# First half of the second FFN: 13 of 22 f-tiles by seven products of block sums in place of eight

## The chip, the core and the metric

One core of one Trainium2 chip runs the kernel. The metric is device time in microseconds, from one launch. The core has five engines that run side by side, each through its own instructions in a fixed order: TensorE (PE, matmuls and transposes; its weight loads are listed as PEld), VectorE (DVE), ScalarE (ACT), GpSimd (POOL) and SyncE (SP), which here only issues DMA transfers. Engines wait for each other by semaphores.

## The reference

The kernel computes one layer of a diffusion backbone on 512 latent tokens and 256 context tokens of width 1024. The change lies in its last part, the second feed-forward layer on the latent tokens, all in fp32:

```python
def ffn_sublayer(h, m, i, w_up, w_down):
    shift, scale, gate = sub_mod(m, i)
    y = swiglu(modulate(h, shift, scale), w_up, w_down)
    return post_ln(DEEPNORM_ALPHA * h + 0.5 * gate * y, ln_g[i], ln_b[i])

def swiglu(u, w_up, w_down):
    a, b = jnp.split(u @ w_up, 2, axis=-1)
    return (jax.nn.silu(a) * b) @ w_down
...
x = post_ln(DEEPNORM_ALPHA * x + gate_x * branch_merge(...), ln_g[1], ln_b[1])
...
x = ffn_sublayer(x, mod_x, 2, ffn2_w_in, ffn2_w_out)
```

`modulate` is a layer norm with scale and shift. The hidden width is D_FF = 2816, which is 22 f-tiles of 128.

## The kernel before

Every fp32 matrix product is made of three products of rounded parts: `split` makes of a tile a high part (a cast to fp32r on ACT) and a low part (the difference, on DVE), and a product is high x high + high x low + low x high. So a product over 1024 channels is 8 x 3 = 24 matmuls with a 128x128 weight tile held still and the tokens moving.

The part around the change runs like this. The output projection w_o of the mixers is a call of `down` (line 186) over four token tiles t of 128; behind the last matmul of each token tile `finish2` (L1319) scales the result by the gate, adds ALPHA times the residual x1, which it loads from the DRAM tensor x1d into a tile xr (L1321, two buffers), applies a layer norm with weights (`post_ln`, L248 and L249) and keeps the result as x2 in SBUF, four tiles. Then `ln_norm` makes from x2 the normalised y(t): statistics on DVE, the power on POOL (L104, L108, L123), the scaling on ACT (L124). `u3` transposes y(t) on PE (`to_u`, L139), adds scale and shift on ACT (L142) and splits it into the token columns of uxh and uxl, the moving operand of the second FFN.

The first half of the second FFN then runs f-tile by f-tile: two weight tiles of 128x1024 (one for a, one for b) are loaded by `Stream`, split, and used by `ffn_unit` (24 matmuls each, then silu and product in `glu`, then the split of the result into hh and hl). The first NH = 4 f-tiles run in two halves of 256 tokens, so that PE can begin when the first two token tiles are there: first the lower half of all four, in between `u3` for token tiles 2 and 3, then the upper halves. The other 18 run with 512 tokens. The second half of the FFN, `down` again, takes hh and hl as still operands and the rows of w_down as moving ones; after it come gate, residual x2 and the last layer norm, token tile by token tile.

The order of instructions on each engine is set when the kernel is built: a scheduler of the tile framework orders the program by its own estimates of cost, and each engine then runs its list strictly in that order. Buffers of one name are handed out again when the last reader of the old contents is done.

Of the kernel before, what the change touches and what calls it, by code (L numbers as in the profile page):

```python
# [17 lines left out]
P = 128  # L18
D = 1024
# [38 lines left out]
def body(ctx, tc, I, out, dbg=None):  # L58
# [73 lines left out]
    def to_u(tp, pp, xn, uh, ul, c0, scale, shift):  # L132

        u32 = tl(tp, [P, KT, P], "u32")
        for hb in range(2):
            ps = tl(pp, [P, 4, P], "ps", 8)
            for q in range(4):
                k = hb * 4 + q
                T.transpose(ps[:, q, :], xn[:, k * P:(k + 1) * P], ident)  # L139
# [4 lines left out]
            split(u32[:, ks], uh[:, ks, c0:c0 + P], ul[:, ks, c0:c0 + P])  # L144

# [40 lines left out]
    def down(pp, ws, hs, ntt, kl, pre=(), between=None, after=None, pieces=0, post=()):  # L186
# [6 lines left out]
        def one(i, t, wh, wl, cols=((0, 0, 512), (1, 0, 512)), first=None, last=None):  # L193
            hh, hl = hs[i]
            if first is None:
                first, last = done[t] == 0, done[t] == len(hs) - 1
                done[t] += 1
            sl = slice(t * P, (t + 1) * P)
            for j, (a, b) in enumerate(((hh, wh), (hh, wl), (hl, wh))):
                for d, c0, c1 in cols:  # L200
                    T.matmul(banks[t][d][:, c0:c1], a[:, sl], b[:, d * 512 + c0:d * 512 + c1], start=first and j == 0, stop=last and j == 2)  # L201

        n = len(hs) - len(pre) - len(post)
# [47 lines left out]
    def ffn_unit(tp, pp, A, B, uh, ul, n, hh, hl):  # L251
# [4 lines left out]
        glu(tp, pa, pb, n, hh, hl)  # L256

    def glu(tp, pa, pb, n, hh, hl):
        s = tl(tp, [P, NX], "fs", 2)
        S.activation(s[:, 0:n], pa[:], AF.Silu)  # L260
        V.tensor_tensor(s[:, 0:n], s[:, 0:n], pb[:], ALU.mult)  # L261
        split(s[:, 0:n], hh[:, 0:n], hl[:, 0:n])
# [37 lines left out]
    def secs(col, s):  # L300
        return col[:, s * 8:s * 8 + 8]
# [988 lines left out]
    PMB[:] = "pm", 4  # L1290
    wb, close_wb = pool("w3", "right")
# [18 lines left out]
    x2p, close_x2p = pool("x2")  # L1310
    x2 = [tl(x2p, [P, D], f"x2{t}") for t in range(4)]
    up, close_up = pool("u3")
    uxh = tl(up, [P, KT, NX], "uxh", 1, F32R)
    uxl = tl(up, [P, KT, NX], "uxl", 1, F32R)
    lp, close_lp = pool("l3")
# [3 lines left out]
    def finish2(t, banks):  # L1319
        xr = tl(lp, [P, D], "xr", 2)  # L1320
        nc.sync.dma_start(xr[:], x1d[t])  # L1321
        h = x2[t]
        for d in range(2):
            sl = slice(d * 512, (d + 1) * 512)
            V.tensor_tensor(h[:, sl], banks[d][:], gx[:, sl], ALU.mult)
            V.scalar_tensor_tensor(h[:, sl], xr[:, sl], ALPHA, h[:, sl], op0=ALU.mult, op1=ALU.add)
        post_ln(lp, h, lng, lnb)
        if "x2" in dbg:
            nc.sync.dma_start(dbg["x2"][t * P:(t + 1) * P, :], h[:])
        y = tl(lp, [P, D], "y1", 2)  # L1330
        ln_norm(lp, y[:], h, act=True)
        return y

    def u3(t, y):
        to_u(lp, pp, y, uxh, uxl, t * P, secs(colx, 7), secs(colx, 6))
# [9 lines left out]
    JU, FU = 2, (1, 3)  # L1345
# [5 lines left out]
    NH = 4  # L1351
    h2a, close_h2a = pool("h2a", "right")
    wc, close_wc = pool("w4", "right")
    hs = []
    key = lambda j: ("", "", "b", "b", "b", "b", "c", "c")[j] if j < 2 * NH else "" if j % 6 in (1, 2) else "b"
    src = [I["up2"][i] for i in range(2 * NF)] + rows(I["dn2"], range(NF))
    ws = Stream(wp, [(w, key(j)) if key(j) else w for j, w in enumerate(src)], WB, 2)
    ws.extra = {"b": (wb, 4, wp, WB), "c": (wc, 2, wp, WB)}
# [7 lines left out]
    hh0 = [h2(h2a, NH) for _ in range(NH)]  # L1366
# [8 lines left out]
    close_wc()  # L1375
    close_lp()
    hp2, close_hp2 = pool("h2", "right")
# [3 lines left out]
    close_tp()  # L1381
    close_up()
# [3 lines left out]
    lng, lnb = load_ln(lp, 2)  # L1386
    PIECES = 2
    banks, _ = down(pp, ws, hs, 4, KL2, pieces=PIECES)
    for t in range(4):
        h = tl(lp, [P, D], "h4", 2)  # L1390
        n, m = (512, D) if t < 3 else (D // PIECES, 512)
        st = tl(lp, [P, PIECES, 6], "bst", 4)
        for i, c in enumerate(range(0, D, n)):
            sl = slice(c, c + n)
            V.tensor_tensor(h[:, sl], banks[t][c // 512][:, c % 512:c % 512 + n], gx[:, sl], ALU.mult)
            V.scalar_tensor_tensor(h[:, sl], x2[t][:, sl], ALPHA, h[:, sl], op0=ALU.mult, op1=ALU.add)
            V.bn_stats(st[:, i, :], h[:, sl])
# [6 lines left out]
        for c in range(0, D, m):  # L1404
            sl = slice(c, c + m)
            V.scalar_tensor_tensor(h[:, sl], h[:, sl], rs[:, 0:1], lnb[:, sl], op0=ALU.mult, op1=ALU.add)
            nc.sync.dma_start(out[t * P:(t + 1) * P, sl], h[:, sl])
    close_lp()
    close_hp2()
    close_h2a()  # L1410
    close_wb()
    close_x2p()
# [102 lines left out]
```

## Time and profile before

| | us |
|---|---|
| median of 3 runs (1559.4 to 1562.53) | 1561.29 |
| the profiled execution | 1563.3 |
| its span, first to last instruction | 1561.2 |
| mean granted clock of TensorE, of full speed | 0.984 |
| w_o by `down`, first L201 matmul at | 1141.5 |
| second FFN, lower and upper halves of four f-tiles, from | 1187.6 |
| the other 18 f-tiles, from | 1236.4 |
| the down projection, from | 1432.3 |

A row of a view in order of time has the start, the duration, the engine, the line, the operation, what it writes and reads with shapes, how many instructions were merged (x2), and in brackets how long the engine was idle before it and which instruction ended that. A row of busy time by stretches has the stretch, its length, then busy time and instruction count of PE, PEld, DVE, ACT and POOL, the granted clock, the share of DMA time and GB/s. Names are those of the program without buffer numbers and trailing digits (u32 is shown as u, x2 as x). A matmul's duration counts its way through the array; in a stream, the distance between starts is what one costs.

### The profile page before, as it was taken

The page shows a single profiled execution, that of the slowest core. Times are in us where ns is not written, and L with a number is a line of the kernel's source. Part 1 is how long each engine was busy: PE and PEld are TensorE (multiplying, and loading weights), DVE is VectorE, ACT ScalarE, POOL GpSimd, SP SyncE. Part 2 cuts the span into 40 slices and gives each one's busy share as a digit, 9 for nine tenths or more (in the row PEclk, how much of TensorE's full clock was granted, in tenths as well). Part 3 has the DMA queues.
Part 4 walks back from the last instruction along what each step waited for, and adds up shares of the span by engine and source line. Part 5 has one row for each costly group of instructions (what it writes and reads, how often), then busy time and mean ns, then how long its engine had stood idle before and what let it go on. Part 6 is the DMA issues. An engine that isn't in the chain of part 4 may idle for free.

```text
span 1561.2 us, 22187 instructions
## 1 busy us (share of the span) xinstructions
PE 1488.2 (95%) x8681; PEld 1252.0 (80%) x8681; DVE 932.0 (60%) x1567; ACT 569.0 (36%) x941; POOL 199.8 (13%) x236
## 2 busy tenths in 40 slices
PE   6999999999999999999996899999799999999997
PEld 4778988888888888889875788867579988888886
DVE  7666762587545487758777795576578333333226
ACT  5434321222112255555543444265426322222110
POOL 1000000000000022223301001376432000000001
PEclk9999999999999999999998999999999999999999
DMA  8665562556555434222476634272252322323221
GB/s 314 201 212 193 181 197 94 196 182 204 195 183 187 164 108 146 85 85 83 137 221 169 172 92 119 88 281 95 90 180 95 96 95 96 103 99 135 95 81 54
DMA packets 106427, 226.43 MB, mean 145 GB/s; under 512 B 34049, under 2 KB 47697, under 8 KB 106321
## 3 DMA queue, kind: packets, MB, share of 16 engines
q1 hardware_dynamic: 105888, 223.89, 43.9%
q8 instruction: 68, 1.11, 0.3%
q10 hardware_dynamic: 434, 1.12, 0.2%
q14 instruction: 37, 0.30, 0.1%
HBM read 204.23 MB, written 20.75 MB: 144 GB/s over the span
## 4 chain that ended last, share of the span: by engine, by line
PE 65%; DMA 12%; DVE 11%; issue 6%; ACT 3%; POOL 2%; SPq 1%; DVEq 0%; POOLq 0%; ACTq 0%
PE ps L201 20%; PE ps L184 8%; PE ps L182 8%; PE ps L183 8%; DMA wr<-in_w_adaT_dram 7%; PE pm L182 4%; PE pm L183 4%; PE pm L184 4%; DVE wl L130 3%; PE pc L842 2%; DVE adap L268 2%; PE po L1250 1%; DMA Dt<-gcd 1%; PE pt L1239 1%; DVE bt L939 1%
## 5 line engine op out<-in xcount | busy, mean ns | idle before, releaser
L130 DVE TENSOR_TENSOR wl<-wr,wh 128x1024 fp32r<-128x1024 f32 (+1 forms) x233 | 283.5, 1220 | 277.6 <-ACT wh L129 274.9
L129 ACT CAST wh<-wr 128x1024 fp32r<-128x1024 f32 (+1 forms) x233 | 237.0, 1021 | 509.6 <-PE ps L183 156.2
L184 PE MATMUL ps<-uxh,wl 128*128 128x512 f32 (+1 forms) x760 | 284.2, 375 | 4.9 <-DVE wl L130 4.9
L182 PE MATMUL ps<-uxh,wh 128*128 128x512 f32 (+1 forms) x760 | 284.5, 376 | 3.3 <-ACT wh L129 3.3
L183 PE MATMUL ps<-uxl,wh 128*128 128x512 f32 (+1 forms) x760 | 283.0, 373 | 0.0
L268 DVE SCALAR_TENSOR_TENSOR adap<-wr,crow 128x1024 f32<-128x1024 f32 x112 | 136.9, 1223 | 88.2 <-DMA wr<-in_w_adaT_dram 86.9
L184 PEld LDWEIGHTS ps<-uxh,wl 128*128 128x128 f32 x760 | 143.7, 189 | 33.6 <-DVE wl L130 8.5
L182 PEld LDWEIGHTS ps<-uxh,wh 128*128 128x128 f32 x760 | 143.7, 189 | 30.3 <-ACT wh L129 5.9
L183 PEld LDWEIGHTS ps<-uxl,wh 128*128 128x128 f32 x760 | 144.1, 190 | 24.2
L104 POOL TENSOR_SCALAR ve<-bmv 128x1 f32<-128x1 f32 x30 | 18.6, 620 | 962.3 <-DVE bmv L116 612.9
L182 PE MATMUL pm<-uxh,wh 128*128 128x512 f32 x320 | 134.0, 419 | 3.6 <-ACT u L142 1.9
L184 PE MATMUL pm<-uxh,wl 128*128 128x512 f32 x320 | 128.5, 401 | 0.7 <-DVE wl L130 0.7
L183 PE MATMUL pm<-uxl,wh 128*128 128x512 f32 x320 | 128.1, 400 | 0.0
L182 PE MATMUL ps<-uch,wh 128*128 128x256 f32 x352 | 98.6, 280 | 0.0
L184 PE MATMUL ps<-uch,wl 128*128 128x256 f32 x352 | 98.3, 279 | 0.0
L183 PE MATMUL ps<-ucl,wh 128*128 128x256 f32 x352 | 98.3, 279 | 0.0
L201 PE MATMUL ps<-wh,hx 128*128 128x512 f32 x352 | 94.8, 389 | 0.0
L261 DVE TENSOR_TENSOR fs<-fs,ps 128x256 f32<-128x256 f32 (+1 forms) x67 | 37.9, 566 | 70.1 <-PE ps L184 70.1
L201 PEld LDWEIGHTS ps<-wh,hx 128*128 128x128 f32 x352 | 65.9, 188 | 13.6
L182 PEld LDWEIGHTS pm<-uxh,wh 128*128 128x128 f32 x320 | 62.1, 194 | 16.0 <-ACT spill L594 2.5
L184 PEld LDWEIGHTS pm<-uxh,wl 128*128 128x128 f32 x320 | 61.8, 193 | 15.2 <-DVE wl L130 1.6
L183 PEld LDWEIGHTS pm<-uxl,wh 128*128 128x128 f32 x320 | 62.0, 194 | 10.7
(329 smaller groups left out, 2636.9 us busy)
## 6 DMA issues: line engine op xcount, KB each, us to landing
wr<-in_up_dram SPq DMA_DIRECT2D x98, 512.0 KB, 3.3
wr<-in_w_adaT_dram SPq DMA_DIRECT2D x88, 512.0 KB, 4.3
wr<-in_dn_dram SPq DMA_DIRECT2D x58, 512.0 KB, 3.6
wr<-in_win_dram SPq DMA_DIRECT2D x52, 512.0 KB, 3.8
wr<-in_w_o_dram SPq DMA_DIRECT2D x8, 512.0 KB, 3.4
ac<-in_up_dram SPq DMA_DIRECT2D x6, 512.0 KB, 5.7
Dt<-gcd SPq DMA_DIRECT2D x12, 256.0 KB, 5.7
bd<-Bt SPq DMA_DIRECT2D x12, 256.0 KB, 2.5
```

Of the source, the lines that this page charges most:

```text
L104: G.tensor_scalar(ve[:], src, EPS, None, op0=ALU.add)
L129: S.copy(hi, src)
L130: V.tensor_tensor(lo, src, hi.bitcast(F32), ALU.subtract)
L182: T.matmul(ps, a, uh[:, k, :], start=(k == 0), stop=False)
L183: T.matmul(ps, a, ul[:, k, :], start=False, stop=False)
L184: T.matmul(ps, b, uh[:, k, :], start=False, stop=(k == nk - 1))
L201: T.matmul(banks[t][d][:, c0:c1], a[:, sl], b[:, d * 512 + c0:d * 512 + c1], start=first and j == 0, stop=last and j == 2)
L261: V.tensor_tensor(s[:, 0:n], s[:, 0:n], pb[:], ALU.mult)
L268: V.scalar_tensor_tensor(pr[:], raw[:], 1.0, crow, op0=ALU.mult, op1=ALU.mult, accum_out=col[:, c:c + 1])
L842: last[0] = T.matmul(*a, **k).ins
L939: V.tensor_tensor(t[:, 0:c, 0:i + 1], L[:, i:i + 1, 0:i + 1].to_broadcast([P, c, i + 1]), Xt[:, 0:c, 0:i + 1], ALU.mult)
L1239: T.transpose(pt[:, q, :], pr[:, i, q * P:(q + 1) * P], ident)
```

## The change

For 13 of the 22 f-tiles the pair of weight tiles and the tokens are taken as a 2x2 by 2x2 block product: the weights in blocks of (a or b) by (lower or upper 512 channels), the tokens in blocks of (lower or upper 512 channels) by (first or last 256 tokens). The eight block products are replaced by seven products of sums of blocks, each 4 k-tiles x 3 parts = 12 matmuls of 256 columns. The sums of token blocks (t14, t32) are made once, on POOL and by four more splits; the sums of weight blocks are made for each f-tile, three on DVE and one on POOL, and split. The results are put together from PSUM by six additions on DVE and one on POOL.

To make room in SBUF, x2 is written to a DRAM tensor x2d and read back at the end, `finish2` works in place in one buffer xr, the f-tiles from the sixth on are kept as one unsplit fp32 tile each and are split during the down projection (`between`), the down weights get a stream of their own, and three f-tiles (NH) instead of four run in halves, two (NS) with 512 tokens in the old way. Four of the remaining 17 (`eight`) stay with eight products.

```diff
-    x2p, close_x2p = pool("x2")
-    x2 = [tl(x2p, [P, D], f"x2{t}") for t in range(4)]
+    x2d = tl(dp, [4, P, D], "x2d")
...
     def finish2(t, banks):
-        xr = tl(lp, [P, D], "xr", 2)
-        nc.sync.dma_start(xr[:], x1d[t])
-        h = x2[t]
+        x2 = tl(lp, [P, D], "xr")
+        nc.sync.dma_start(x2[:], x1d[t])
         for d in range(2):
             sl = slice(d * 512, (d + 1) * 512)
-            V.tensor_tensor(h[:, sl], banks[d][:], gx[:, sl], ALU.mult)
-            V.scalar_tensor_tensor(h[:, sl], xr[:, sl], ALPHA, h[:, sl], op0=ALU.mult, op1=ALU.add)
-        post_ln(lp, h, lng, lnb)
+            h = tl(lp, [P, 512], "h1")
+            V.tensor_tensor(h[:], banks[d][:], gx[:, sl], ALU.mult)
+            V.scalar_tensor_tensor(x2[:, sl], x2[:, sl], ALPHA, h[:], op0=ALU.mult, op1=ALU.add)
+        post_ln(lp, x2, lng, lnb)
+        nc.sync.dma_start(x2d[t], x2[:])
...
     def u3(t, y):
-        to_u(lp, pp, y, uxh, uxl, t * P, secs(colx, 7), secs(colx, 6))
+        u32s.append(to_u(lp if t < 2 else lp2, pp, y, uxh, uxl, t * P, secs(colx, 7), secs(colx, 6), f"u32{t}"))
+        if t > 1:
+            a, b = u32s[t - 2], u32s[t]
+            lo, hi = slice(0, 4), slice(4, 8)
+            for o, i0, i1 in ((a[:, lo], b[:, lo], a[:, lo]), (b[:, lo], b[:, hi], b[:, lo]), (b[:, hi], b[:, hi], a[:, lo]), (a[:, hi], a[:, hi], b[:, hi])):
+                G.tensor_tensor(o, i0, i1, ALU.subtract)
+            sl = slice((t - 2) * P, (t - 1) * P)
+            for src, (h, l) in ((a, t14), (b, t32)):
+                split(src[:], h[:, :, sl], l[:, :, sl])
...
-    JU, FU = 2, (1, 3)
+    JU, FU = 2, (1, 2)
...
-    for f in range(NH, NF):
-        ffn_unit(tp, pp, ws.get(2), ws.get(2), uxh, uxl, NX, *h2(hp2, NF - NH))
+    def blocks(f):
+        ra, rb = tl(wp, [P, D], "wr", WB), tl(sw, [P, D], "rb", 2)
+        nc.sync.dma_start(rb[:], I["up2"][2 * f + 1])
+        nc.sync.dma_start(ra[:], I["up2"][2 * f])
+        a11, a12, a21, a22 = ra[:, 0:512], ra[:, 512:1024], rb[:, 0:512], rb[:, 512:1024]
...
+        V.tensor_tensor(s[:, 0], a21, a22, ALU.add)
+        V.tensor_tensor(s[:, 1], s[:, 0], a11, ALU.subtract)
+        G.tensor_tensor(a21, a11, a21, ALU.subtract)
+        V.tensor_tensor(s[:, 2], a12, s[:, 1], ALU.subtract)
...
+        split(ra[:], ah[:], al[:])
+        split(s[:, 0], sh[:, 0], sl[:, 0])
+        split(s[:, 1:], sh[:, 1:], sl[:, 1:])
+        split(rb[:], bh[:], bl[:])
...
+    def product(w, i, ps):
+        (wh, wl), (uh, ul) = w[i], moved[i]
+        for k in range(4):
+            a, b = wh[:, k * P:(k + 1) * P], wl[:, k * P:(k + 1) * P]
+            T.matmul(ps[:], a, uh[:, k], start=k == 0, stop=False)
+            T.matmul(ps[:], a, ul[:, k], start=False, stop=False)
+            T.matmul(ps[:], b, uh[:, k], start=False, stop=k == 3)
...
+    def seven(w):
...
+        p = made(1)
+        S.copy(c11, p)
+        p2, p5 = made(2), made(5)
+        S.copy(c22, p5)
+        V.tensor_tensor(c21, c11, made(6), ALU.add)
+        V.tensor_tensor(c11, c11, p2, ALU.add)
+        V.tensor_tensor(c12, c21, c22, ALU.add)
+        V.tensor_tensor(c12, c12, made(3), ALU.add)
+        V.tensor_tensor(c21, c21, made(7), ALU.add)
+        G.tensor_tensor(c22, c21, c22, ALU.add)
+        S.activation(sn[:, 0:2], sn[:, 0:2], AF.Silu)
+        V.tensor_tensor(c21, c21, made(4), ALU.add)
+        V.tensor_tensor(whole().rearrange("p (a n) -> p a n", a=2), sn[:, 0:2], sn[:, 2:4], ALU.mult)
...
+    for f in range(NS):
+        ffn_unit(tp, pp, ws.get(1), ws.get(0), uxh, uxl, NX, *h2(h2a, NH + NS), fs=True)
+    take = lambda f: (eight, plain(f)) if (f - NH - NS) % 4 == 3 else (seven, blocks(f))
+    ready = [take(NH + NS), take(NH + NS + 1)]
+    for f in range(NH + NS, NF):
+        do, w = ready.pop(0)
+        do(w)
+        if f + 2 < NF:
+            ready.append(take(f + 2))
...
+    def between(j):
+        for h in raw[2 * j:2 * j + 2]:
+            split(h, *[t[:] for t in h2(hd, 13)])
...
-    banks, _ = down(pp, ws, hs, 4, KL2, pieces=PIECES)
+    banks, _ = down(pp, ws, hs, 4, KL2, between=between, pieces=PIECES, n=NF)
     for t in range(4):
...
+        x2 = tl(lp, [P, D], "x2", 2)
+        nc.sync.dma_start(x2[:], x2d[t])
```

The first place is SP's list of transfers where w_o is being multiplied. gx, lng and lnb are the gate and the norm's weights, xr is the residual, wr are weight tiles. Before:

```order
L237 DMA gx_10787<-gate_1048 128x1024
L242 DMA lng_10789<-in_ln_g_dram 128x1024
L243 DMA lnb_10790<-in_ln_b_dram 128x1024
L1321 DMA xr_10855<-x1d_4217 128x1024
L1321 DMA xr_10933<-x1d_4217 128x1024
L1321 DMA xr_11034<-x1d_4217 128x1024
L1321 DMA xr_11135<-x1d_4217 128x1024
L164 DMA wr_11199<-in_up_dram 128x1024
L164 DMA wr_11205<-in_up_dram 128x1024
```

With the change:

```order
L1327 DMA xr_10854<-x1d_4217 128x1024
L1334 DMA x2d_10775<-xr_10854 128x1024
L1327 DMA xr_10935<-x1d_4217 128x1024
L1334 DMA x2d_10775<-xr_10935 128x1024
L1327 DMA xr_11039<-x1d_4217 128x1024
L165 DMA wr_11214<-in_up_dram 128x1024
L165 DMA wr_11220<-in_up_dram 128x1024
L165 DMA wr_11226<-in_up_dram 128x1024
L1334 DMA x2d_10775<-xr_11039 128x1024
L165 DMA wr_11373<-in_up_dram 128x1024
L165 DMA wr_11639<-in_up_dram 128x1024
L1327 DMA xr_11143<-x1d_4217 128x1024
```

The four residual loads stood together; now each comes behind the store of the token tile ahead of it, and five weight loads stand between them or ahead of the last.

The second place is PE where the fourth token tile y(3) is transposed. Before (here ps_11362 and ps_11363 are the lower half of the third f-tile, ps_11446 that of the fourth):

```order
L182 MATMUL ps_11363<-uxh_10782,wh_11213 128x256
L183 MATMUL ps_11363<-uxl_10783,wh_11213 128x256
L184 MATMUL ps_11363<-uxh_10782,wl_11214 128x256
L139 MATMUL ps_11424<-ident_64,y_2058_11152 128x128 x4
L139 MATMUL ps_11435<-ident_64,y_2058_11152 128x128 x4
L182 MATMUL ps_11446<-uxh_10782,wh_11219 128x256
```

With the change (ps_11319 is the second f-tile, ps_11410 the third):

```order
L183 MATMUL ps_11319<-uxh_10780,wh_11216 128x256
L184 MATMUL ps_11319<-uxl_10781,wh_11216 128x256
L185 MATMUL ps_11319<-uxh_10780,wl_11217 128x256
L139 MATMUL ps_11380<-ident_64,y_2065_11163 128x128 x4
L139 MATMUL ps_11391<-ident_64,y_2065_11163 128x128 x4
L183 MATMUL ps_11410<-uxh_10780,wh_11222 128x256
```

The transposes moved from behind the third lower half to behind the second.

The third place is POOL between the norms of the fourth token tile. Before, its list there holds only the small steps of the norms (bmv are the statistics, ve, rs and nb what is made of them):

```order
L104 TENSOR_SCALAR ve_2056_11146<-bmv_11144 128x1
L108 TENSOR_TENSOR rs_2057_11148<-ve_2056_11146,mhalf_67 128x1
L104 TENSOR_SCALAR ve_2061_11158<-bmv_11156 128x1
L108 TENSOR_TENSOR rs_2062_11160<-ve_2061_11158,mhalf_67 128x1
L123 TENSOR_SCALAR nb_11162<-bmv_11156,rs_2062_11160 128x1
```

With the change (u are the token tiles ahead of their split):

```order
L1351 TENSOR_TENSOR u_2039_10986<-u_2104_11287,u_2039_10986 128x512
L1351 TENSOR_TENSOR u_2104_11287<-u_2104_11287 128x512
L104 TENSOR_SCALAR ve_2063_11156<-bmv_11154 128x1
L1351 TENSOR_TENSOR u_2104_11287<-u_2104_11287,u_2039_10986 128x512
L108 TENSOR_TENSOR rs_2064_11158<-ve_2063_11156,mhalf_67 128x1
L1351 TENSOR_TENSOR u_2039_10986<-u_2039_10986,u_2104_11287 128x512
L104 TENSOR_SCALAR ve_2068_11169<-bmv_11167 128x1
L108 TENSOR_TENSOR rs_2069_11171<-ve_2068_11169,mhalf_67 128x1
L123 TENSOR_SCALAR nb_11173<-bmv_11167,rs_2069_11171 128x1
```

Four subtractions of 128x512 now stand among the small steps.

More of the change, by code (lines that the diff above doesn't have):

```diff
@@ L195, in one @@
             if first is None:
-                first, last = done[t] == 0, done[t] == len(hs) - 1
+                first, last = done[t] == 0, done[t] == nk - 1
                 done[t] += 1
@@ L1365, in body @@
     w0 = []
-    hh0 = [h2(h2a, NH) for _ in range(NH)]
+    hh0 = [h2(h2a, NH + NS) for _ in range(NH)]
     for i in range(2):
@@ new lines, in body, with made @@
+    hc = [tl(h2a, [P, NX], "hr")[:]]
+    def seven(w):
+        sn = tl(tp, [P, 4, 256], "sn", 2)
+        def made(i):
+            ps = tl(pp, [P, 256], "ps", 8)
+            product(w, i, ps)
+            return ps[:]
+        c11, c12, c21, c22 = [sn[:, j] for j in range(4)]
+        p = made(1)
[11 more added lines that the diff above has]
+        V.tensor_tensor(whole().rearrange("p (a n) -> p a n", a=2), sn[:, 0:2], sn[:, 2:4], ALU.mult)
@@ new lines, in whole, with plain @@
+    def whole():
+        if not hc:
+            c = tl(wb, [P, D], "wh" if len(hs) // 2 % 2 else "wl", 4)
+            hc.extend((c[:, 0:NX], c[:, NX:]))
+        hs.append(hc.pop(0))
+        return hs[-1]
+    def plain(f):
+        w = []
+        for j, (rp, rn, p, n) in enumerate(((wp, "wr", wp, ("wh", "wl")), (sw, "rb", sw, ("bh", "bl")))):
+            raw = tl(rp, [P, D], rn, 2)
+            nc.sync.dma_start(raw[:], I["up2"][2 * f + j])
+            w.append([tl(p, [P, D], x, 2, F32R) for x in n])
+            split(raw[:], *[x[:] for x in w[-1]])
+        return w
```

78 lines of the change are left out of this document (56 added, 22 removed).

## The prediction

> **What bounds the kernel now.** I read the page first, then the busy time by stretches, then single rows in order of time around the point where the second FFN begins.
>
> ```profile
> span 1561.2 us, 22187 instructions
> PE 1488.2 (95%) x8681; PEld 1252.0 (80%) x8681; DVE 932.0 (60%) x1567; ACT 569.0 (36%) x941; POOL 199.8 (13%) x236
> PE 65%; DMA 12%; DVE 11%; issue 6%; ACT 3%; POOL 2%; SPq 1%; DVEq 0%; POOLq 0%; ACTq 0%
> ...
> 1187.50:1236.40 48.90, 48.08 (x402) 47.84 (x401) 27.37 (x40) 27.02 (x48) 4.76 (x7) 1.00 0.35 114
> 1236.40:1432.30 195.90, 195.90 (x867) 162.20 (x866) 66.71 (x72) 56.57 (x74) 0.00 (x0) 1.00 0.30 98
> 1432.30:1551.30 119.00, 119.00 (x527) 98.54 (x526) 42.36 (x48) 18.45 (x18) 5.54 (x6) 1.00 0.26 89
> ```
>
> The last three rows are the stage that changes. From 1187.5 to 1236.4 four f-tiles run in two halves of 256 tokens, from 1236.4 to 1432.3 the other eighteen run with 512 tokens, and from 1432.3 the down projection runs. PE is busy all the time at clock 1.00, while DVE works for 67 of 196 us. So up to 1551 time here is the number of matmuls times their spacing, and nothing else shows.
>
> ```profile
> 1194.78 0.28 PE L182 MATMUL ps<-uxh,wh 128*128 128x256 f32 x1
> ...
> 1205.58 0.28 PE L184 MATMUL ps<-uxh,wl 128*128 128x256 f32 x1
> 1206.68 1.09 PE L139 MATMUL ps<-ident,y 128*128 128x128 f32 x8 [0.82 <-ACT y L124]
> ...
> 1236.40 0.40 PE L182 MATMUL ps<-uxh,wh 128*128 128x512 f32 x1
> ...
> 1432.27 0.61 PE L201 MATMUL ps<-wh,hh 128*128 128x512 f32 x2
> ```
>
> Between the first two rows lie 90 steps of 256 columns: 10.80 us, 0.120 us each. Between the last two lie 18 x 48 = 864 matmuls of 512 columns: 195.87 us, 0.2267 us each. The third row is the one place in the stage where PE stood still, 0.82 us, for the fourth normalised token tile y(3).
>
> **What the change takes away.** An f-tile with eight products has 48 matmuls of 512 columns, 48 x 0.2267 = 10.88 us; one with seven has 7 x 4 x 3 = 84 of 256 columns, 84 x 0.120 = 10.08 us. Thirteen of them save 13 x 0.80 = 10.4 us. Three f-tiles instead of four run in halves; the one that moves costs 10.88 instead of 96 x 0.120 = 11.52, 0.6 us less. The sum is 11.0 us less for PE.
>
> Here a rule of the Trainium skill differs from the row: "TensorE: Matmul & The Clock Gate", section "Back-to-back issue gap", has N/2.4 + 2.5 ns for an isolated matmul, which would be 109 ns and 216 ns, and a seven-product tile would save 1.2 us instead of 0.8, the whole 15.4 + 0.1 us instead of 11.0. The rows have 120 and 227 ns, and the measurement decides.
>
> **What it adds beside PE.** A seven-product tile needs on DVE three splits of 1024 columns (first weight, second weight, two sums together), five operations of 512 (three sums, one split, the product with silu) and six of 256 columns from PSUM or SBUF.
>
> ```profile
> L130 DVE TENSOR_TENSOR wl<-wr,wh x35: 1217/1225/1226, 1242.9 to 1427.9; 128x1024 fp32r<-128x1024 f32 x35
> L130 DVE TENSOR_TENSOR hl<-fs,hh x17: 683/685/687, 1249.5 to 1423.6; 128x512 fp32r<-128x512 f32 x17
> ...
> 1202.48 0.42 DVE L261 TENSOR_TENSOR fs<-fs,ps 128x256 f32<-128x256 f32 x1
> ...
> L1303 POOL TENSOR_TENSOR yb<-yb,gt x8: 1271/1702/2254, 1120.8 to 1144.5; 128x512 f32<-128x512 f32 x8
> ...
> 1134.15 1.67 POOL L1303 TENSOR_TENSOR yb<-yb,gt 128x512 f32<-128x512 f32 x1 [1.83 <-DVE gt L1302]
> ...
> 1134.59 1.77 DVE L130 TENSOR_TENSOR wl<-wr,wh 128x512 fp32r<-128x512 f32 x1
> ```
>
> That is 3 x 1.225 + 5 x 0.685 + 6 x 0.42 = 9.6 us. POOL adds one subtraction of 512 and one sum of 256 columns, at 1.27 us for 512 about 1.9 us. The last two rows overlap, and the DVE split takes 1.77 instead of 0.685 us: POOL and DVE shut each other out there, so I put all of POOL's 1.9 us on DVE, 11.5 us for a seven. An eight-product tile needs 2 x 1.225 + 0.685 = 3.1 us (its output is split later). A group of three sevens and an eight is 37.6 us of DVE against 3 x 10.08 + 10.88 = 41.1 us of PE. Weights are made two tiles ahead, so this is hidden: 0. If the cover goes, see the third rival.
>
> The deferred splits stand at the start of the down projection: 13 on DVE (13 x 0.685 = 8.9 us) ahead of the third down weight (1.2 us), 10.1 us, while PE has two tiles of 24 x 0.2267 x 2 = 10.9 us. Hidden with under 1 us to spare; 0 taken, 2 us if not. The x2 tiles that come back from DRAM at the end are issued during the down matmuls: 0, at most one load.
>
> **What it adds on the path: one buffer for x1d.** Until now the four loads xr<-x1d were issued one behind another. Now x2 is built in place in the one xr buffer, and the load of token tile t+1 waits on SP until ACT has made y(t) out of it. Queued behind that wait are the weights of the second and third f-tile, and behind y(t) everything that makes token columns. PE stands in order: the transposes of y(3) come before the third f-tile's first half. What one round costs is in these rows.
>
> ```profile
> 1157.05 1.29 DVE L1326 SCALAR_TENSOR_TENSOR x<-xr,x 128x512 f32<-128x512 f32 x2 [3.25 <-DMA xr<-x1d]
> ...
> 1165.82 1.28 DVE L1326 SCALAR_TENSOR_TENSOR x<-xr,x 128x512 f32<-128x512 f32 x2
> ...
> 1176.98 1.28 DVE L1326 SCALAR_TENSOR_TENSOR x<-xr,x 128x512 f32<-128x512 f32 x2
> ...
> 1188.75 0.68 DVE L1326 SCALAR_TENSOR_TENSOR x<-xr,x 128x512 f32<-128x512 f32 x1
> ...
> 1167.19 1.24 ACT L124 ACTIVATE y<-x,nb,rs 128x1024 f32<-128x1024 f32 x1 [19.80 <-POOL nb L123]
> 1175.44 1.24 ACT L124 ACTIVATE y<-x,nb,rs 128x1024 f32<-128x1024 f32 x1 [2.32 <-POOL nb L123]
> 1188.72 1.24 ACT L124 ACTIVATE y<-x,nb,rs 128x1024 f32<-128x1024 f32 x1
> 1205.38 1.24 ACT L124 ACTIVATE y<-x,nb,rs 128x1024 f32<-128x1024 f32 x1 [1.10 <-POOL nb L123]
> ...
> wr<-in_up_dram SPq DMA_DIRECT2D x98, 512.0 KB, 3.3
> ...
> xr<-x1d SPq DMA_DIRECT2D x4, 512.0 KB, 6.4
> ```
>
> From the first use of xr to the end of y it took 11.4, 10.9, 13.0 and 17.9 us; the later ones are longer because weight splits stand between on DVE. A lone load of the same size lands in 3.3 us (the 6.4 of xr is with seven loads in flight). I keep y(0) at 1168.4. Round 1: 10.9, plus two steps that hold one half buffer (0.6 each) and two token splits now in between (1.2): 13.3. Round 2: 13.0 plus three more weight splits and two such steps, less what POOL's small steps hide: 17.3. Round 3 loses weight splits, but on POOL three of the four new subtractions stand ahead of the rsqrt it needs: 17.5, near the 17.9 of before. With three loads, y(3) = 1168.4 + 9.9 + 48.1 = 1226.4, 19.8 us later than the 1206.6 of before, and PE needs it one half tile earlier. PE reaches that place at about 1213 and waits some 13 us. Its earlier waits (for the columns of y(1), y(2)) end before 1213 and cost nothing more.
>
> From there: 1.1 us for eight transposes, then 4 halves, 4 x 5.76 = 23.0 us, then 6 x 10.88 + 13 x 10.08 = 196.3 us, up to 1446.8.
>
> ```profile
> 835.00:840.00 5.00, 0.00 (x0) 0.00 (x0) 0.36 (x1) 1.78 (x1) 0.00 (x0) 0.87 0.83 162
> 840.00:845.00 5.00, 0.00 (x0) 0.00 (x0) 4.02 (x21) 0.63 (x1) 1.16 (x6) 0.50 0.73 168
> 845.00:850.00 5.00, 2.33 (x36) 1.98 (x37) 2.87 (x13) 1.61 (x4) 1.83 (x4) 0.50 0.62 152
> 850.00:855.00 5.00, 5.00 (x53) 3.36 (x56) 4.69 (x15) 1.54 (x2) 2.08 (x5) 0.76 0.44 125
> ```
>
> After a standstill of this length the granted clock is 0.50 and comes back some 5 us after work does: about 5 us at half speed, 2.5 us lost. So the up stage ends at about 1449.3 instead of 1432.3: **17 us later**, and the rest stays as it is. The profiled execution took 1563.3 us (span 1561.2 and 2.1 around it), 2.0 over the median of 1561.3; the difference goes onto the median: 1578.
>
> Bounds of the unknown term: if nothing in between costs anything, a round is 10.9 + 3.3 and y(3) comes at 1211.0, which gives -0.9 us, or +1.6 with the clock. If the loads take the 6.4 us of the xr row, three times 3.1 us more: 1587.
>
> **Rivals.** First, the rounds are short or hidden, and PE's count rules: 1550. It decides if a round of load and normalisation is under about 11 us, so that y(3) is there at 1201; no row of the 10.9 to 17.9 us leaves room for a load, so this needs the load to start before y is done. Price: 11.0 us less. Second, the rounds are at their floor, 14 to 15 us each, and eat the gain: 1560 to 1564. The four rows speak against it, two of them being longer by themselves. Third, DVE becomes the bound of the sevens: their work rises over (41.1 - 3.1) / 3 = 12.7 us each; at 13.5 a group takes 43.6 instead of 41.1 us, and four groups add 10 us to my sum: 1588 and over. For it speaks that 11.5 us a seven is more than PE's 10.08, so three sevens in a row lag by over 4 us; against it, that the lead is two tiles. The Trainium skill, "SBUF — State Buffer", section "Who interferes with whom", says that a DVE instruction with two SBUF inputs and a GpSimd instruction that reads SBUF block each other whole; by that rule, the trace agrees (1.77 instead of 0.685 us).
>
> **How the numbers follow.** Forecast 0.68 (1568 to 1588), first rival 0.13, second 0.10, third 0.09. The predicted time is 1578. The range from 1562 to 1590 leaves out the first rival and most of the third. A measurement of this kernel tells about 0.2%, 3 us, from no change. Slower holds the forecast, the third and a little of the second: 0.79; the same 0.07; faster 0.14.
>
> **What would show it.** Right: xr loads issued at about 1168, 1185 and 1206, each behind an ACT row of y; PE waiting over 10 us ahead of the transposes of the fourth token tile and a clock of 0.50 behind it; 256-column matmuls at 0.120 us with no wait in the sevens, the stretch from the first full f-tile to the first down matmul near 196 us for nineteen tiles. Wrong: y(3) before 1212, or PE waiting for DVE inside the sevens, or for the third down weight.

## The result, and the profile after

The changed kernel takes 1580.87 us (median of 4 runs, 1578.17 to 1583.5) against 1560.35 us of the kernel before beside it (4 runs, 1557.89 to 1562.53): 1.0132 times as long, 95% interval 1.0107 to 1.0157. It is slower, and the forecast of 1578 us lies 3 us below. One of the ten executions of f1_two_late, an experiment below, took 1837 us at a granted clock of 0.75 and is left out of its time.

The page of the changed kernel, in its first lines and its chain of waits:

```profile
span 1576.4 us, 23359 instructions
PE 1480.2 (94%) x9101; PEld 1263.3 (80%) x9101; DVE 1027.3 (65%) x1712; ACT 601.3 (38%) x995; POOL 247.8 (16%) x270
...
PE 62%; DMA 15%; DVE 12%; issue 5%; ACT 3%; POOL 2%; SPq 1%; DVEq 0%; POOLq 0%; ACTq 0%
```

PE is busy 8.0 us less than before (1480.2 against 1488.2), although the span is 15.2 us longer. So the seven products save PE time, and something else costs about three times as much. Where PE stands still is in the list of its waits, from w_o to the end of the program (engine, tile, line, whom it waits for: us in total, times, longest):

```profile
PE ps L139 <- ACT y L124: 14.9, 1, 14.9
PE ps L183 <- ACT uxh L129: 6.9, 1, 6.9
PE ps L184 <- DVE uxl L130: 2.0, 1, 2.0
```

Three waits, all before the second FFN has all its token columns, and none in the f-tiles with seven products (the sevens; those with eight are the eights) or at the down projection. The transfers of xr in order of time on SP's queue, and the ACT rows that make y:

```profile
1149.22 0.42 SPq L1327 DMA_DIRECT2D xr<-x1d  x1
...
1167.12 0.32 SPq L1327 DMA_DIRECT2D xr<-x1d  x1
...
1183.86 0.32 SPq L1327 DMA_DIRECT2D xr<-x1d  x1
...
1203.30 0.33 SPq L1327 DMA_DIRECT2D xr<-x1d  x1
```

```profile
1165.85 1.25 ACT L124 ACTIVATE y<-xr,nb,rs 128x1024 f32<-128x1024 f32 x1 [18.90 <-POOL nb L123]
...
1223.97 1.24 ACT L124 ACTIVATE y<-xr,nb,rs 128x1024 f32<-128x1024 f32 x1 [4.92 <-POOL nb L123]
```

The second load goes out at 1167.12, the moment y(0) is done (1165.85 + 1.25), and so on round by round, to y(3) at 1225.2. Over the four tiles DVE stood 16.2 us behind these loads, as the view of the tile xr has it; 2.9 of them lie ahead of the first tile, where the kernel before stood 3.25 us as well:

```profile
DMA xr<-x1d: 16.2, 4
...
DMA to landing us min/median/max: 2.6/2.6/4.1
```

The last three rows to read are PE's, in order of time, at the borders of the stage: the transposes of y(3), the first full f-tile, the first down matmul.

```profile
1225.26 0.69 PE L139 MATMUL ps<-ident,y 128*128 128x128 f32 x2 [14.94 <-ACT y L124]
...
1251.53 0.39 PE L183 MATMUL ps<-uxh,wh 128*128 128x512 f32 x1
...
1446.07 0.62 PE L202 MATMUL ps<-wh,hh 128*128 128x512 f32 x2
```

**How lengths are compared here.** The first matmul of w_o (L201, L202) begins between 1133.0 and 1145.1 us in the profiled executions of these kernels, although PE has the same matmuls ahead of it in all of them; two executions of one and the same program, g1_two_eights and h2_again, lie 2.8 us apart there. That scatter is as large as some of the effects, so stages are measured from that matmul: 1141.54 before, 1141.37 after. The table gives them for all kernels, worked out from the starts of PE rows.

| kernel | w_o to transposes of y(3) | w_o to first full f-tile | full f-tiles | w_o to down | time, us | against before |
|---|---|---|---|---|---|---|
| before | 65.1 | 94.9 | 195.9 (18) | 290.7 | 1560.35 | |
| changed | 83.9 | 110.2 | 194.5 (19) | 304.7 | 1580.87 | 1.0132 |
| e1_two_xr | 67.2 | 92.3 | 194.6 | 286.9 | 1556.1 | 0.9977 (0.9964 to 0.9989) |
| e8_before_single | 80.2 | 109.9 | 195.9 (18) | 305.8 | 1573.07 | 1.0102 (1.0072 to 1.0131) |
| e2_all_eight | 85.5 | 110.7 | 208.8 | 319.4 | 1585.63 | 1.0171 (1.0155 to 1.0186) |
| e4_defer | 85.3 | 110.6 | 194.5 | 305.2 | 1577.29 | 1.011 (1.0088 to 1.0131) |
| f1_two_late | 66.9 | 90.1 | 194.5 | 284.7 | 1555.75 | 0.9977 (0.9958 to 0.9995) |
| f2_two_late_dve | 64.9 | 88.2 | 194.5 | 282.7 | 1553.51 | 0.9971 (0.9955 to 0.9986) |
| e3_all_seven | 85.3 | 111.6 | 194.0 | 305.6 | 1578.4 | 1.0124 (1.0095 to 1.0153) |
| f3_nogap | 84.3 | 110.9 | 196.4 | 307.3 | 1576.4, one run | |
| h1_gap128 | 83.7 | 110.0 | 196.6 | 306.6 | 1582.32, one run | |
| g1_two_eights | 65.0 | 88.4 | 191.3 | 279.7 | 1552.32 | 0.9956 (0.9941 to 0.997) |
| h2_again | 66.1 | 88.8 | 191.5 | 280.3 | 1550.45, one run | |

Between before and changed, the way to the first full f-tile grows by 15.3 us, the full f-tiles shrink by 1.3 us (there is one more of them), and the down projection, from its first to its last matmul, takes 121.0 instead of 119.5 us. That is 15.5 us; the two profiled executions differ by 14.9 (1578.17 and 1563.3).

### The profile page after: what moved, and what is told of

Same layout as the page of the kernel before. It is cut to its first block, busy times and chain, and to the rows that moved or that the text cites. A ratio compares the mean times of both kernels' runs of the same rounds, so it can differ in the third digit from the quotient of the medians.

```text
span 1576.4 us, 23359 instructions
## 1 busy us (share of the span) xinstructions
PE 1480.2 (94%) x9101; PEld 1263.3 (80%) x9101; DVE 1027.3 (65%) x1712; ACT 601.3 (38%) x995; POOL 247.8 (16%) x270
## 4 chain that ended last, share of the span: by engine, by line
PE 62%; DMA 15%; DVE 12%; issue 5%; ACT 3%; POOL 2%; SPq 1%; DVEq 0%; POOLq 0%; ACTq 0%
PE ps L202 17%; DMA wr<-in_w_adaT_dram 7%; PE ps L185 5%; PE ps L183 5%; PE ps L184 5%; PE pm L183 5%; PE pm L184 5%; PE pm L185 5%; PE ps L1437 3%; DVE wl L130 3%; PE ps L1436 3%; PE ps L1435 3%; PE pc L844 2%; DVE adap L270 2%; DMA wr<-in_up_dram 1%
## 5 line engine op out<-in xcount | busy, mean ns | idle before, releaser
L130 DVE TENSOR_TENSOR wl<-wr,wh 128x1024 fp32r<-128x1024 f32 (+1 forms) x216 | 261.5, 1215 | 191.2 <-ACT wh L129 190.2
L129 ACT CAST wh<-wr 128x1024 fp32r<-128x1024 f32 (+1 forms) x216 | 218.7, 1017 | 362.6 <-PE ps L202 87.6
L183 PE MATMUL ps<-uxh,wh 128*128 128x512 f32 (+1 forms) x504 | 190.2, 378 | 11.7 <-ACT uxh L129 6.9
L270 DVE SCALAR_TENSOR_TENSOR adap<-wr,crow 128x1024 f32<-128x1024 f32 x112 | 136.9, 1223 | 89.7 <-DMA wr<-in_w_adaT_dram 88.2
L185 PE MATMUL ps<-uxh,wl 128*128 128x512 f32 (+1 forms) x504 | 188.9, 375 | 3.9 <-DVE wl L130 3.8
L184 PE MATMUL ps<-uxl,wh 128*128 128x512 f32 (+1 forms) x504 | 188.1, 374 | 2.0 <-DVE uxl L130 2.0
L183 PEld LDWEIGHTS ps<-uxh,wh 128*128 128x128 f32 x504 | 97.0, 193 | 30.4 <-ACT wh L129 7.5
L185 PEld LDWEIGHTS ps<-uxh,wl 128*128 128x128 f32 x504 | 96.8, 192 | 23.9 <-DVE wl L130 7.8
L184 PEld LDWEIGHTS ps<-uxl,wh 128*128 128x128 f32 x504 | 97.0, 192 | 17.3 <-DVE uxl L130 2.3
L202 PE MATMUL ps<-wh,hx 128*128 128x512 f32 x352 | 94.8, 389 | 0.0
L202 PEld LDWEIGHTS ps<-wh,hx 128*128 128x128 f32 x352 | 65.9, 188 | 13.6
L185 PEld LDWEIGHTS pm<-uxh,wl 128*128 128x128 f32 x320 | 61.5, 192 | 15.2 <-DVE wl L130 1.8
L129 ACT CAST hx<-fs 128x512 fp32r<-128x512 f32 x22 | 13.6, 620 | 149.8 <-DVE fs L263 149.8
L184 PEld LDWEIGHTS pm<-uxl,wh 128*128 128x128 f32 x320 | 61.8, 193 | 10.7
```

The source lines that it names most:

```text
L129: S.copy(hi, src)
L130: V.tensor_tensor(lo, src, hi.bitcast(F32), ALU.subtract)
L183: T.matmul(ps, a, uh[:, k, :], start=(k == 0), stop=False)
L184: T.matmul(ps, a, ul[:, k, :], start=False, stop=False)
L185: T.matmul(ps, b, uh[:, k, :], start=False, stop=(k == nk - 1))
L270: V.scalar_tensor_tensor(pr[:], raw[:], 1.0, crow, op0=ALU.mult, op1=ALU.mult, accum_out=col[:, c:c + 1])
```

## Experiments

**Theory 1**: the loss is the reload into the one xr buffer, which strings the four token tiles behind each other. **Rival A**: the rounds are long because of the new splits and subtractions on DVE and POOL. **Rival B**: DVE holds the sevens, so the gain never came.

**e1_two_xr**: a second buffer for xr. Room for it comes from the tile h1, whose place y takes, and from fs, which is halved (that line is not shown); all else as changed.

```diff
-        x2 = tl(lp, [P, D], "xr")
+        x2 = tl(lp, [P, D], "xr", 2)
         nc.sync.dma_start(x2[:], x1d[t])
+        y = tl(lp, [P, D], "y1", 2)
...
-            h = tl(lp, [P, 512], "h1")
-            V.tensor_tensor(h[:], banks[d][:], gx[:, sl], ALU.mult)
-            V.scalar_tensor_tensor(x2[:, sl], x2[:, sl], ALPHA, h[:], op0=ALU.mult, op1=ALU.add)
+            V.tensor_tensor(y[:, sl], banks[d][:], gx[:, sl], ALU.mult)
+            V.scalar_tensor_tensor(x2[:, sl], x2[:, sl], ALPHA, y[:, sl], op0=ALU.mult, op1=ALU.add)
```

> The changed kernel with two xr buffers: room for the second is made by using the y tile for the product of bank and gate (so h1 goes) and by halving fs. The seven-product tiles are as they are. Theory 1, the stall is the reload that waits for the tile's only buffer: the loads are issued with two tiles in flight, no load waits for the y just before it, and y(3) ends at 1207 to 1214 instead of 1225.2; PE waits 5 to 12 us there instead of 14.9, and not at all for uxh and uxl before; the time falls by 12 to 19 us, to 1562 to 1569. Rival, the rounds are long because of the splits and subtractions that now stand on DVE and POOL between two normalisations: y(3) stays at 1218 or later and the time at 1573 to 1581.

In order of time, SP's transfers of xr, and PE at y(3) and at the first down matmul:

```profile
1145.00 1.01 SPq L1327 DMA_DIRECT2D xr<-x1d  x2
...
1163.95 0.32 SPq L1327 DMA_DIRECT2D xr<-x1d  x1
...
1171.93 0.32 SPq L1327 DMA_DIRECT2D xr<-x1d  x1
```

```profile
1204.46 0.69 PE L139 MATMUL ps<-ident,y 128*128 128x128 f32 x2 [9.05 <-ACT y L124]
...
1424.17 0.62 PE L202 MATMUL ps<-wh,hh 128*128 128x512 f32 x2
```

The loads run ahead again, the waits for uxh and uxl are gone, and the one for y(3) is 9.05 us. From w_o to the first down matmul it takes 17.8 us less than the changed kernel. The time, 1556.1 us, is lower than the 1562 to 1569 I gave: in the profiled execution w_o began 4.1 us earlier, a scatter that I had not allowed for. It is even 0.2% faster than the kernel before. The store to x2d and the reload at the end are still in this kernel, so they are not the loss. Theory 1 holds, rival A falls as the main cause.

**e8_before_single**: the kernel before with the single in-place buffer, the store to x2d and the reload at the end, and nothing else.

```diff
-        xr = tl(lp, [P, D], "xr", 2)
+        xr = h = tl(lp, [P, D], "xr")
         nc.sync.dma_start(xr[:], x1d[t])
-        h = x2[t]
...
+        nc.sync.dma_start(x2d[t], h[:])
```

> The kernel before, with only this of the change: x2 is built in place in a single xr buffer, stored to DRAM, and loaded again for the last layer norm; all 22 f-tiles keep eight products, and there are no subtractions on POOL. Theory 1 (single buffer): y(3) ends at 1219 to 1226 instead of 1206.6, PE waits 12 to 19 us before its transposes, and the time rises by 13 to 22 us, to 1574 to 1583. Rival (the rounds are long because of the new splits and subtractions): PE waits under 6 us more and the time is under 1567.

Its list of PE's waits, from w_o to the end of the up stage:

```profile
PE ps L182 <- ACT uxh L129: 7.5, 1, 7.5
PE ps L139 <- ACT y L124: 3.5, 2, 2.9
PE ps L183 <- DVE uxl L130: 2.5, 1, 2.5
```

The way to the first down matmul grows by 15.1 us, the time by 14.3. So the single buffer alone, without a seven and without a subtraction on POOL, brings nearly the whole loss. I had expected 12 to 19 us of waiting ahead of y(3); there are only 2.9 there, because PE had already lost 10.0 us ahead of it, waiting for the columns of the second token tile, y(1), and because this kernel puts one more half f-tile in front of y(3). The down projection takes 119.4 us with x2 reloaded from DRAM, as before: that reload costs nothing.

**e2_all_eight**: `take = lambda f: (eight, plain(f))`.

> The changed kernel with eight products in all 17 late f-tiles; stall, buffers and deferred splits stay. Theory 1 (the sevens run at PE's own spacing and save all they should): 13 tiles go from about 10.03 back to 10.88 us, the time rises by 11 us to 1592. Rival (DVE and POOL hold the sevens, so that part of the saving never came): it rises by under 6 us, to below 1587.

The full f-tiles take 208.8 instead of 194.5 us: 14.2 us for 13 tiles, 1.09 us each, more than I expected. By the time alone, 1585.63 us, the rival would have won; w_o began at 1133.0 here, 8.4 us earlier than in the changed kernel, and that hides the difference. The stage decides: rival B falls, the sevens save what they should and more. Why more, f3_nogap below tells.

**e4_defer**: the subtractions and splits for t14 and t32 taken out of `u3` and written behind, in the upper halves.

> The changed kernel with the four subtractions on POOL and the splits of t14 and t32, for both late token tiles, issued behind the third token tile's last step, in the upper halves, instead of right behind the columns of their token tile. The xr buffer stays single. Theory 1 (single buffer, with POOL's subtractions ahead of the last rsqrt a small part of the third round): y(3) ends 2 to 6 us earlier than 1225.2, the time is 1574 to 1579. Rival (the subtractions and splits make the rounds long): y(3) ends before 1215 and the time is below 1570. If the work piles up ahead of the first seven instead, PE waits there for t14 or t32 and the time is above 1582.

This told nothing apart. The scheduler of the framework hoisted them back to the same place. In order of time, POOL in e4_defer:

```profile
1214.40 0.21 POOL L104 TENSOR_SCALAR ve<-bmv 128x1 f32<-128x1 f32 x1 [0.76 <-DVE bmv L116]
1214.69 2.22 POOL L1351 TENSOR_TENSOR u<-u,u 128x512 f32<-128x512 f32 x1
1216.87 0.74 POOL L108 TENSOR_TENSOR rs<-ve,mhalf 128x1 f32<-128x1 f32 x1
```

and in the changed kernel:

```profile
1213.52 0.21 POOL L104 TENSOR_SCALAR ve<-bmv 128x1 f32<-128x1 f32 x1 [0.76 <-DVE bmv L116]
1213.82 2.22 POOL L1351 TENSOR_TENSOR u<-u,u 128x512 f32<-128x512 f32 x1
1216.00 0.74 POOL L108 TENSOR_TENSOR rs<-ve,mhalf 128x1 f32<-128x1 f32 x1
```

The subtraction stands between ve and rs in both, and takes 2.22 us there. What the norm loses by it is seen on DVE, in the changed kernel: a split of 128x256 beside the subtraction took 1.48 us (0.41 us for one at 1208.53, with POOL idle), and then DVE stood idle for 0.46 us until rs came. What the subtractions cost in all had to be tried in another way (f2_two_late_dve).

**f1_two_late**: e1_two_xr, with the transposes of y(3) behind all three lower halves (`u3(3, ys[3])` after the last of them).

> The kernel of e1_two_xr, and the transposes of y(3) stand on PE behind the lower halves of all three f-tiles instead of behind two. In e1_two_xr PE still stood 9.05 us there. Theory (what is left of the stall is that y(3) is wanted one half f-tile earlier than in the kernel before): 5.76 us of matmuls go into that wait, 3 to 4 us of it stay, and from the start of w_o to the first down matmul it takes 5 to 7 us less than the 286.9 of e1_two_xr; time 1548 to 1552. Rival (y(3) moves back as much as PE's work, since the splits and silu steps of the third half then stand ahead of it on DVE and ACT): less than 2 us gained, 1554 and over.

PE in order of time:

```profile
1206.94 0.55 PE L139 MATMUL ps<-ident,y 128*128 128x128 f32 x3 [3.45 <-ACT y L124]
...
1211.11 0.58 PE L183 MATMUL ps<-uxh,wh 128*128 128x256 f32 x1 [3.07 <-ACT uxh L129]
```

The wait at y(3) falls from 9.05 to 3.45 us, as expected, but only 2.2 us are gained. Neither theory nor rival: y(3) stayed where it was, and a new wait of 3.07 us stands behind the transposes. ACT needs 2.9 us for the scale and shift (L142) and a cast after them (L129) before the upper halves can begin, and the half f-tile that I moved forward had covered just that. What PE may do before y(3) and what it may do during these ACT steps is the same work, and can be spent only once.

**f2_two_late_dve**: the eight subtractions of token blocks on DVE (`V.tensor_tensor` for `G.tensor_tensor`).

> The kernel of f1_two_late, with the eight subtractions of the token blocks on DVE instead of POOL. Theory (POOL's subtractions stand ahead of the small steps of the last norm and hold DVE up as well): y(3) ends 2 to 4 us earlier, the rest of the wait goes, 2 to 4 us less than f1_two_late. Rival (it is all the same who does them, since each then stands ahead of the norm on DVE): within 1 us of f1_two_late. The third round would be longer on DVE by at most 4 x 0.69 = 2.8 us.

y(3) comes 2.0 us earlier from w_o, its wait falls to 1.49 us, and the way to down is 1.9 us shorter, just under the 2 to 4 us expected. A DVE step of y(3)'s norm shows part of it, with the POOL row beside it, first in f1_two_late, then in f2_two_late_dve:

```profile
1195.68 2.30 DVE L251 SCALAR_TENSOR_TENSOR xr<-xr,rs,lnb 128x1024 f32<-128x1024 f32 x1 [0.76 <-POOL rs L108]
...
1195.62 1.29 POOL L1350 TENSOR_TENSOR u<-u 128x512 f32<-128x512 f32 x1
```

```profile
1197.33 1.28 DVE L251 SCALAR_TENSOR_TENSOR xr<-xr,rs,lnb 128x1024 f32<-128x1024 f32 x1
```

Beside a POOL subtraction that had begun 0.06 us before it, the step took 2.30 instead of 1.28 us. So rival A is a real term, some 2 us of it, beside some 15 of the single buffer (e8_before_single).

**e3_all_seven**: `take = lambda f: (seven, blocks(f))`.

> The changed kernel with seven products in all 17 late f-tiles; stall and buffers stay. In the changed kernel a seven took PE 9.89 us and an eight 10.99, and no wait stood between them. Theory 1 (DVE and POOL have room): all 17 run at 9.89 us, from the first 512-column matmul to the first down matmul 190.2 us instead of 194.5. Rival (the eights are the room that DVE needs, the third rival of the prediction): PE waits for weights inside the sevens, and the stretch takes 195 us or more.

The stretch is 194.0 us, nearer the rival. Two PE rows in it, one seven apart, and DVE and POOL rows of the seven before:

```profile
1421.39 0.39 PE L1435 MATMUL ps<-t32h,sh 128*128 128x256 f32 x1 [0.51 <-DVE sn L1456]
...
1432.08 0.39 PE L1435 MATMUL ps<-t32h,sh 128*128 128x256 f32 x1 [0.53 <-DVE sn L1456]
```

```profile
1412.83 1.22 DVE L130 TENSOR_TENSOR sl<-s,sh 128x1024 fp32r<-128x1024 f32 x1
1413.09 1.56 POOL L1461 TENSOR_TENSOR sn<-sn 128x256 f32<-128x256 f32 x1 [6.29 <-DVE sn L1460]
1414.68 0.42 DVE L1463 TENSOR_TENSOR sn<-sn,ps 128x256 f32<-128x256 f32 x1 [0.63 <-POOL sn L1461]
...
1415.84 1.62 POOL L1415 TENSOR_TENSOR rb<-wr,rb 128x512 f32<-128x512 f32 x1 [1.19 <-DVE s L1412]
1416.22 2.32 DVE L130 TENSOR_TENSOR bl<-rb,bh 128x1024 fp32r<-128x1024 f32 x1
```

The tiles come 10.69 us apart, at the pace of DVE. The two DVE splits have the same shape and both lie beside a POOL operation; what differs is which begins first. At sl it is DVE: the split takes 1.22 us, as without POOL, and POOL's sum of 256 columns takes 1.56 us, against 0.74 us where DVE is idle (changed kernel, 1426.66). At bl it is POOL, and the split takes 2.32 us. So POOL costs DVE 1.1 us at bl and a wait of 0.63 us at L1463 in each seven. The first listed wait of PE stands only in the twelfth seven, later than the tenth that the expectation of g1_two_eights below puts down; from there five sevens take 10.6 to 10.7 us instead of 9.89, of which 2.5 us in all are listed as waits. So a seven needs about 10.7 us on DVE, and the four eights are the slack that keeps DVE off the path.

**f3_nogap** and **h1_gap128**: the small tiles ahead of uxh and of the t tiles taken out (0 bytes), or made 128 bytes instead of 64. These gaps are part of the change, though the lines shown of it leave them out. In f3_nogap the small tiles behind (192 bytes) go as well, so what is allocated above them moves too; in h1_gap128 they shrink, and only uxh, uxl and the t tiles move.

```diff
-    tl(up, [P, 16], "gap")
...
-    tl(up2, [P, 16], "gap")
```

> The changed kernel without the four small gap tiles around uxh, uxl and the t tiles, so that these tiles begin 64 bytes lower; nothing else moves on any engine. Theory (the place of the moving operand in SBUF sets the spacing): 256-column matmuls of the sevens go from 0.1178 back to about 0.120 us and the 512-column ones of the eights from 0.2288 back to about 0.2267; from the first 512-column matmul to the first down matmul 194.5 + 2.4 - 0.6 = 196.3 us. Rival (the spacing comes from the order of the operands or from the weights): it stays within 0.3 us of 194.5.

> The changed kernel with the gap tiles ahead of uxh and of the t tiles at 128 bytes instead of 64 (the ones behind them shrink, so nothing else moves). With 64 bytes the sevens ran at 0.1178 us per 256-column matmul and the eights at 0.2288 per 512, without the gaps at 0.1200 and 0.2273. If the place within a longer row decides, a third pair of values comes out: sevens below 0.1178 or eights between the two. If only being off the old place counts, the values are those of 64 bytes, 9.89 and 10.98 us per f-tile.

PE rows at the start of the first seven, of the first eight, and of the next seven, of f3_nogap and then of the changed kernel:

```profile
1269.66 0.28 PE L1431 MATMUL ps<-uxh,wh 128*128 128x256 f32 x1
...
1299.89 0.40 PE L183 MATMUL ps<-uxh,wh 128*128 128x512 f32 x1
...
1310.80 0.28 PE L1431 MATMUL ps<-uxh,wh 128*128 128x256 f32 x1
```

```profile
1273.51 0.28 PE L1435 MATMUL ps<-uxh,wh 128*128 128x256 f32 x1
...
1303.19 0.39 PE L183 MATMUL ps<-uxh,wh 128*128 128x512 f32 x1
...
1314.17 0.28 PE L1435 MATMUL ps<-uxh,wh 128*128 128x256 f32 x1
```

Three sevens (252 matmuls) take 30.23 us without the gaps and 29.68 with them, 0.1200 and 0.1178 us a matmul; an eight takes 10.91 and 10.98. At 128 bytes it is 29.90 and 11.20. So the spacing changes with the place of the moving operand in SBUF, each place has its own pair of values in these runs (one execution each of f3_nogap and h1_gap128), and 64 bytes is the best of the three here, by 1.9 us over the stage. The place is not all: g1_two_eights has another value at 64 bytes.

**g1_two_eights** and **h2_again**: f2_two_late_dve with `(f - NH - NS) % 6 == 5`, two eights among the last 17 f-tiles, and the same program once more.

> The kernel of f2_two_late_dve with two f-tiles of eight products among the last 17 (the sixth and the twelfth) instead of four. With all 17 as sevens the tiles came 10.67 us apart once the lead was used up, from the tenth on: that is what DVE needs for a seven, against 9.89 us on PE. Theory (DVE needs 10.67 us per seven and 3.1 per eight): 15 x 10.67 + 2 x 3.1 = 166.3 us of DVE against 15 x 9.89 + 2 x 10.99 = 170.3 us of PE, so nothing waits in the sevens and the stretch from the first 512-column matmul to the first down matmul falls from 194.5 to 192.3 us; the time falls by 2 us against f2_two_late_dve. Rival (five sevens in a row outrun the lead of two tiles): PE waits for DVE near the end of each row of five, and the stretch stays at 194 us or more.

> The kernel of g1_two_eights unchanged, run again. There the first two rows of five sevens ran at 0.1133 us per matmul and the last five at 0.1179. If that belongs to the program (its places in SBUF, which go round with the buffers), the same rows show the same spacings; if it belongs to the execution, the spacings lie elsewhere or are all 0.1178.

The stretch is 191.3 us (192.3 expected) and the time 1552.32 us, 0.9956 of the kernel before: this version beats both. DVE's count held, though PE did wait three times, 1.6 us in all, at the end of the second row of five. PE ran faster there than I had reckoned, which fits that it outran DVE. Starts of the first seven, the first eight, the matmul with the first wait, the last five sevens, and the first down matmul:

```profile
1251.19 0.28 PE L1436 MATMUL ps<-uxh,wh 128*128 128x256 f32 x1
...
1298.79 0.39 PE L183 MATMUL ps<-uxh,wh 128*128 128x512 f32 x1
...
1353.26 0.39 PE L1436 MATMUL ps<-t32h,sh 128*128 128x256 f32 x1 [1.16 <-DVE sn L1457]
...
1371.02 0.28 PE L1436 MATMUL ps<-uxh,wh 128*128 128x256 f32 x1
...
1420.48 0.62 PE L202 MATMUL ps<-wh,hh 128*128 128x512 f32 x2
```

The first five take 47.60 us (420 matmuls, 0.1133 us), the last five 49.46 (0.1178). In h2_again they took 47.60 and 49.43, so the second execution repeats the pattern nearly, but neither answer of the expectation is the whole of it. In both, the spacing goes from 0.113 to 0.118 us inside the tenth seven, at the first wait (1353.26 here), though uxh, uxl and the t tiles stay where they are. In h2_again the first of the last five sevens ran at 0.113 us once more, up to a stop of 0.07 us, and the other four at 0.118. So two spacings occur with the moving operands at the same places, and in these two executions a stop of PE is where 0.113 changes to 0.118.

## Why the prediction was right

- **The path of y(3): right, and the cause is shown.** Forecast were loads at 1168, 1185 and 1206 and y(3) at 1226.4; the rows say 1167.1, 1183.9, 1203.3 and 1225.2. e1_two_xr takes the loss away and e8_before_single brings it alone. Rivals one and two of the prediction (rounds hidden, rounds at their floor) needed y(3) at 1201, or rounds of 14 to 15 us; the rounds are 16.7, 19.4 and 21.9 us. Forecast were 16.6, 20.6 and 20.8 (each with 3.3 for its load); that the errors of the last two cancel is luck. One reading of the prediction was wrong: in the kernel before, the third and fourth load wait for a buffer too (issued at 1158.4 and 1167.1), but only for the addition that reads it (L1326), not for y. The single in-place buffer puts off that release.
- **"Waits about 13 us": near.** PE waited 14.94 us there, as it reached the place at 1210.3 and not 1213, and 8.9 us before that for the columns of y(1). I had taken the earlier waits as free, since PE would have stood at y(3) anyway, and so they were.
- **After y(3): right.** Forecast 1.1 + 23.0 + 2.5 = 26.6 us to the first full f-tile, measured 26.3. The clock by stretches of 5 us (busy time of PE, PEld, DVE, ACT and POOL, then the granted clock):

```profile
1220.00:1225.00 5.00, 0.00 (x0) 0.00 (x0) 2.62 (x5) 1.03 (x1) 1.03 (x3) 0.50 0.23 95
1225.00:1230.00 5.00, 4.74 (x22) 4.74 (x23) 0.14 (x1) 3.79 (x11) 1.28 (x1) 0.50 0.00 0
1230.00:1235.00 5.00, 5.00 (x40) 5.00 (x39) 1.37 (x3) 1.78 (x3) 4.12 (x3) 0.88 0.00 0
```

  It stays at 0.50 up to 1230 and, as a mean of 0.88 in the next 5 us says, about 1.2 us longer if it then goes to 1.00 at once: about 6 us of work, where 5 were forecast.
- **PE's saving: right in kind, its size was off.** The term "13 x 0.80 = 10.4 us" took 0.120 us a matmul from rows of the kernel before. The sevens took 9.89 us (29.68 / 3), not 10.08, and full tiles with eight products 10.98, not 10.88: 194.5 us for the stretch where 196.3 were forecast. f3_nogap gives 196.4, so the difference is the gap tiles, an edit whose effect the prediction left at nothing. The Trainium skill, "TensorE: Matmul & The Clock Gate", section "Back-to-back issue gap", has 109 ns for an isolated matmul of 256 columns; here 113 to 120 ns were measured in streams.
- **DVE hidden: right.** No wait stands in the sevens. I had 11.5 us per seven, with all of POOL's time on DVE; e3_all_seven shows 10.7. The limit of 12.7 us per seven, for three sevens and an eight, was not reached, so the third rival did not come. That POOL and DVE shut each other out is seen in the groups of the changed kernel, two DVE operations of one shape and two SBUF inputs, the first beside a POOL operation in all eleven rows, the second in one:

```profile
L1413 DVE TENSOR_TENSOR s<-s,wr 128x512 f32<-128x512 f32 x11 | 18.2, 1653 | 0.0
...
L1416 DVE TENSOR_TENSOR s<-wr,s 128x512 f32<-128x512 f32 x11 | 8.0, 729 | 0.1
```

  The Trainium skill, "SBUF — State Buffer", section "Who interferes with whom", gives the rule that such an operation and a GpSimd instruction that reads SBUF hold each other off; the trace agrees, 1653 against 729 ns.
- **Deferred splits, third down weight, reload of x2: hidden, as forecast.** No wait of PE stands there.
- **"The rest stays as it is": not quite.** The down projection took 121.0 us instead of 119.5, in the changed kernel and in every kernel made from it, with no wait. Matmul groups there took 1.40 instead of 1.36 us for six, in some weight tiles and not in others. Another place of the operands would fit, but that was not tried; the cause stays open.

The errors in PE's saving and in the down projection, -1.8 and +1.5 us, nearly cancel, which is luck; the way to the first full f-tile grew by 15.3 us where the steps gave 16.6. The stage rows therefore give +15.5 us where I had +17. The medians give +20.5. The 5 us between lie in executions that were not profiled: the scatter ahead of w_o is large enough for them, but that they lie there is not shown.

## What to carry to other kernels

When a change buys SBUF by giving up a second buffer, look at what that buffer kept in flight: here one 4 KB buffer less put load, norm and scaling of four tiles in a row, and cost as much as 13 f-tiles of saved products brought (15.1 us in e8_before_single, 14.2 in e2_all_eight). Room can be found elsewhere (a tile that is written later anyway took the place of h1, and fs was twice as wide as needed). Compare stages from a common instruction when the time ahead of them scatters by more than the effect, and see in the instruction order whether a moved line did move.

## What the runs showed of the hardware that was not expected

- The spacing of matmuls at a granted clock of 1.00 changes with the place of the moving operands in SBUF: uxh, uxl and the t tiles moved by 0, 64 and 128 bytes gave 0.1200, 0.1178 and 0.1187 us at 256 columns and 0.2273, 0.2288 and 0.2333 us at 512. What is best for the one width is not best for the other.
- At one place (64 bytes) two spacings occur. In g1_two_eights nine sevens and the tenth up to its first wait ran at 0.1133 us a matmul, the rest of it and the last five at 0.1178, with the moving operands at the same places; h2_again has the same change at the same wait and a second one at a stop of 0.07 us. What sets the two apart was not found.
- Of a DVE operation with two SBUF inputs and a POOL operation that overlap, the one that began first kept its time and the other was held: in e3_all_seven a POOL sum took 1.56 us behind a DVE split that kept its 1.22 us (0.74 us with DVE idle), and in f1_two_late a DVE step took 2.30 us behind a POOL subtraction that kept its 1.29 us (1.28 us without).
